# The delta net's 16 triangular systems substituted in two halves of eight, value units and doublings pinned between the steps

## The chip, the cores and the metric

The kernel runs on one core of one Trainium2 chip. A core has TensorE (PE, the matrix products; PEld is its weight load), VectorE (DVE), ScalarE (ACT), GpSimd (POOL) and SyncE (SP, which issues the loads). The engines run side by side and each works its own list of instructions strictly in order; an instruction that needs another engine's result waits on a semaphore, and everything behind it in its list waits too. The metric is the time of one execution on the device in microseconds (us), median of several runs.

## The reference, cut to what matters

Two blocks of a language model over 256 tokens of width 1024. The first has a state-space mixer and a mixture of experts; the second has four layers: attention with forget gates, gated linear attention, a gated delta net, and attention again. The change lies in the delta net alone:

```
qkv = silu(causal_conv(xn @ w_in))          # q, k: 4 heads of 128; v: 8 heads of 128
q = l2_norm(q) * d ** -0.5;  k = l2_norm(k)
tri = where(strict, (k*beta) @ k.T * decay, 0) + eye(64)     # per head and chunk of 64 tokens
u = triangular_solve(tri, v*beta);  w = triangular_solve(tri, k*beta*exp(gc))
# then a scan over the chunks, an RMS norm, a gate silu(z) and the output projection
```

The kernel treats the 256 tokens of a head as two blocks of 128, so there are 8 heads x 2 = 16 triangular systems of 128 x 128. Each needs an inverse.

## The kernel before, in words

Weights are streamed through a ring of six 1 MB slots in SBUF (`s.ring`). A unit of 256 output columns is split into a high and a low part (`split_unit`: ACT's cast at L247, DVE's subtraction at L248) and multiplied in three products per 128 rows and columns (`dense`, L277): 48 products of 128x256 per unit. The delta net (`gdn`, from L1458) takes its weights as such units: keys and queries (2, 0, 3, 1), values (4 to 7), the gate z (8, and a last one of 256 columns).

- `unit` (L1500) is one dense unit followed by a causal convolution of four taps and a silu (`conv_silu`: padding L352, ACT's first tap L356, six DVE steps L360, gating L365).
- `l2` (L1504) normalises keys and queries: sums by products with ones (L1510), inverse roots in 13 small steps (`rsqrt`, on POOL here), eight transposes that spread the roots (L1520), two scalings on DVE (L1522).
- `systems` (L1543) makes, for two groups of four systems, the key and query products (L1550), the decays (L336, L338 on PE, exponentials L343 on ACT) and the masked matrices U (L1560, L1561).
- `compact` (L1586) takes the 8x8 blocks of the diagonals out of U on DVE (L1589, L1591).
- `substitute` (L1593) inverts all 8x8 blocks of all 16 systems at once: ACT and POOL write the columns out wide (L1601), PE transposes them in seven transposes (L1604), DVE works seven steps of a product and a reduction (L1609, L1610), PE transposes back (L1612), ACT copies (L1613).
- `spread` (L1615) sets the blocks on the diagonals of Tm (L1618) and its transpose Vm by flips (L1581, copies L1621).
- `lower`, `update`, `flipped` (L1630 to L1660) double the size of the inverted blocks three times, 8 to 64. A level of a group of four systems is four products (L1636), a masked copy X on DVE (L1642), four products (L1654), an addition on DVE (L1655) and, on the first two levels, a flip (L1581) with a copy (L1660). The twelve level-and-group steps run as a pipeline, `lower` two ahead of `update` and three ahead of `flipped`.
- `queries` (L1537) multiplies the queries' decays by their products on DVE (L1539, L1540); `v_turn` (L1669) transposes the convolved values (L1672).

The program's text is not the order of the engines' lists. A scheduler with a timeline of its own sets the order of all instructions after their dependencies; `s.tc.issue_after(x)` is a further condition by which the instructions in it come behind x. In the order that it made, all four value units stand ahead of the second half's `systems` on PE.

## Time and profile before

| | us |
|---|---|
| median of 3 runs (1290.63 to 1292.61) | 1292.08 |
| profiled execution | 1291.23 |
| its span | 1289.6 |
| PE busy (88% of the span) | 1134.1 |
| DVE busy (46%) | 589.9 |
| ACT busy (38%) | 491.4 |
| POOL busy (11%) | 137.6 |
| mean granted TensorE clock, share of full | 0.965 |

The delta net takes the span from about 980 to 1155 us; `l2`, `systems`, the substitution and the doubling stand between 1003 and 1094. Shares over the whole span say little of such a stage; it is read from windows, from the timeline of an engine and from the chain of work that ended last. In a timeline, a row gives the start and the duration of a group of equal instructions, and in brackets for how long the engine was idle before it and whose result ended that. Instructions overlap by some 0.08 us on DVE, and matmuls are pipelined, so the time that one takes from the next is the distance of their starts.

### The profile page before, as it was taken

Reading aid. Unit: us, or ns where it says so; the run is one execution under the profiler, and the core shown is the slowest. Engines: PE = TensorE matmul, PEld = TensorE weight load, DVE = VectorE, ACT = ScalarE, POOL = GpSimd, SP = SyncE. Lnnn points to the kernel's source line nnn. Section 1 sums busy time; section 2 is a strip of 40 time slices with the busy share of each in tenths; the row PEclk is TensorE's granted clock in tenths of the full one; section 3 lists DMA queues with packets and bytes.
Section 4 is the critical chain, followed back from the end, with each engine's and each line's share of the span. In section 5 each row is a group of like instructions: output and inputs, shape, how many; then the busy total and the mean of one; then the engine's idle time right before and its main releaser. Section 6 shows DMA issues by size and latency. Waiting matters only on the chain.

```text
span 1289.6 us, 18973 instructions
## 1 busy us (share of the span) xinstructions
PE 1134.1 (88%) x7458; PEld 845.0 (66%) x7459; DVE 589.9 (46%) x1136; ACT 491.4 (38%) x996; POOL 137.6 (11%) x406
## 2 busy tenths in 40 slices
PE   5999999996778677777777999999999969999998
PEld 4998999741323131322314788989688959897887
DVE  3976776410101010110104565757467777666554
ACT  4554454210101010000104567656455533356763
POOL 2000632000000000000000332010001110012310
PEclk8999999998899898999989999999999979999999
DMA  6843647799999999999999553454335420165620
GB/s 226 290 134 99 191 159 283 280 421 425 421 424 424 425 424 424 425 425 424 425 424 317 171 164 131 166 165 153 112 109 170 138 76 2 34 165 168 158 98 33
DMA packets 126903, 312.72 MB, mean 242 GB/s; under 512 B 7559, under 2 KB 72842, under 8 KB 109530
## 3 DMA queue, kind: packets, MB, share of 16 engines
q1 hardware_dynamic: 126458, 311.26, 65.5%
q8 instruction: 60, 0.98, 0.3%
q0 software_dynamic: 352, 0.20, 0.1%
q14 instruction: 33, 0.27, 0.1%
HBM read 310.39 MB, written 1.05 MB: 242 GB/s over the span
## 4 chain that ended last, share of the span: by engine, by line
PE 39%; DMA 25%; DVE 3%; ACT 2%; issue 1%; POOL 1%; SPq 0%; DVEq 0%; ACTq 0%
PE pd L298 19%; DMA we<-in_w_down 12%; PE pd L277 9%; DMA we<-in_w_gate 6%; DMA we<-in_w_up 6%; DMA w<-in_fox_w_in 2%; DVE wl L248 1%; PE ps L1654 1%; PE ps L1193 1%; PE ps L1581 1%; PE ps L1636 1%; ACT wh L247 1%; PE ps L1211 1%; PE pd L969 1%; DVE cv L360 0%
## 5 line engine op out<-in xcount | busy, mean ns | idle before, releaser
L277 PE MATMUL pd<-x,wh 128*128 128x256 f32 x1744 | 327.6, 288 | 2.3 <-DVE x L161 1.2
L248 DVE TENSOR_TENSOR wl<-w,wh 128x1024 fp32r<-128x1024 f32 (+1 forms) x206 | 251.2, 1223 | 119.0 <-ACT wh L247 117.6
L247 ACT CAST wh<-w 128x1024 fp32r<-128x1024 f32 (+1 forms) x206 | 214.5, 1046 | 203.2 <-PE pd L277 103.8
L277 PEld LDWEIGHTS pd<-x,wh 128*128 128x128 f32 x1744 | 276.7, 194 | 5.5 <-DVE x L161 2.1
L298 PE MATMUL pd<-wh,x 128*128 128x512 f32 (+3 forms) x896 | 249.5, 367 | 6.9 <-ACT x L160 2.4
L277 PE MATMUL pd<-x,wl 128*128 128x256 f32 x872 | 248.8, 287 | 0.8 <-DVE wl L248 0.8
L969 PE MATMUL pd<-we,xt 128*32 128x512 f32 x1012 | 173.2, 681 | 71.9 <-DMA we<-in_w_up 50.6
L298 PEld LDWEIGHTS pd<-wh,x 128*128 128x128 f32 x896 | 159.7, 190 | 33.8 <-ACT wh L247 3.8
L277 PEld LDWEIGHTS pd<-x,wl 128*128 128x128 f32 x872 | 168.7, 194 | 1.6 <-DVE wl L248 1.3
L969 PEld LDWEIGHTS pd<-we,xt 128*32 128x32 f32 x1012 | 40.5, 122 | 195.7 <-DMA we<-in_w_up 86.8
L298 PE MATMUL pd<-wl,x 128*128 128x512 f32 (+3 forms) x448 | 158.3, 366 | 1.5 <-DVE wl L248 1.4
L993 PE MATMUL pd<-we,sq 128*32 128x512 f32 x512 | 98.2, 624 | 27.6 <-DMA we<-in_w_down 21.7
L298 PEld LDWEIGHTS pd<-wl,x 128*128 128x128 f32 x448 | 84.2, 190 | 15.6 <-DVE wl L248 2.9
L1005 DVE TENSOR_TENSOR hT<-hT,ps 128x512 f32<-128x512 f32 x32 | 22.0, 687 | 149.3 <-PE ps L1004 149.3
L993 PEld LDWEIGHTS pd<-we,sq 128*32 128x32 f32 x512 | 24.7, 112 | 94.0 <-issue 45.0
L982 DVE SCALAR_TENSOR_TENSOR cv<-cv,rslot,pd 128x512 f32<-128x512 f32 x8 | 6.0, 747 | 130.9 <-PE pd L969 130.9
L99 POOL TENSOR_SCALAR rq_y<-rs_v 128x8 int32<-128x8 int32 (+2 forms) x24 | 6.4, 266 | 522.8 <-DVE rs_v L192 440.0
L987 ACT COPY sq<-ps 128x512 f32<-128x512 f32 x8 | 4.7, 585 | 149.8 <-PE ps L985 149.8
L999 ACT COPY ys<-pd 128x512 f32<-128x512 f32 x16 | 9.3, 586 | 120.7 <-PE pd L993 120.7
L1316 POOL MEMSET at<- 128x1024 f32 x1 | 1.0, 951 | 434.7 <-PE pd L993 434.7
L980 DVE SCALAR_TENSOR_TENSOR cv<-th,pd 128x512 f32<-128x512 f32 x8 | 5.5, 688 | 85.8 <-ACT th L978 85.8
L978 ACT ACTIVATE th<-pd,rslot 128x512 f32<-128x512 f32 x8 | 5.5, 687 | 90.3 <-PE pd L969 51.3
(492 smaller groups left out, 1374.3 us busy)
## 6 DMA issues: line engine op xcount, KB each, us to landing
we<-in_w_down SPq DMA_DIRECT2D x46, 1024.0 KB, 14.8
we<-in_w_up SPq DMA_DIRECT2D x45, 1024.0 KB, 16.0
we<-in_w_gate SPq DMA_DIRECT2D x43, 1024.0 KB, 14.5
w<-in_fox_w_in SPq DMA_DIRECT2D x30, 1024.0 KB, 6.8
w<-in_w_in SPq DMA_DIRECT2D x22, 1024.0 KB, 7.7
we<-in_w_up SPq DMA_DIRECT2D x38, 512.0 KB, 14.2
we<-in_w_down SPq DMA_DIRECT2D x36, 512.0 KB, 15.8
we<-in_w_gate SPq DMA_DIRECT2D x34, 512.0 KB, 15.6
```

Of the source, the lines that this page charges most:

```text
L247: nc.scalar.copy(h, v[:, k:k + m])
L248: nc.vector.tensor_tensor(l, v[:, k:k + m], h, OP.subtract)
L277: nc.tensor.matmul(acc[:, c], w[k][:, cs], x[:, k, p], start=start and c == 0 and at == 0 and i == 0, stop=stop and at == KC - 1 and i == ...
L298: nc.tensor.matmul(acc[j], x[:, k, p, ts], w[k], start=k == order[0] and i == 0 and (n != T or j == 0), stop=k == order[-1] and i == 2, sk ...
L969: mm = nc.tensor.matmul(out[32 * j:32 * j + 32], xt[:, k, 32 * j:32 * j + 32], w[name, 4 * q + j, k // 4][k % 4], start=k == 0, stop=k == ...
L993: mm = nc.tensor.matmul(py[h][32 * j:32 * j + 32], at[:, f, 32 * j:32 * j + 32], w["w_down", 4 * q + j, f // 2][f % 2][:, 512 * h:512 * h ...
L1005: nc.vector.tensor_tensor(hT[:, 2 * u:2 * u + 2], hT[:, 2 * u:2 * u + 2], pt.rearrange("p (i t) -> p i t", i=2), OP.add)
L1193: nc.tensor.transpose(pt[:, (2 * i + j) * P:(2 * i + j + 1) * P], n4[w, j][:, 2 * o + i], s.ident)
L1211: nc.tensor.matmul(pl[:, P:384], q[:, P:], k, start=False, stop=False, skip_group_check=True)
L1581: nc.tensor.transpose(pt[:, a * P:(a + 1) * P], x[:, a], s.ident)
L1636: nc.tensor.matmul(pt[:, a * P:(a + 1) * P], U[:, 2 * g4 + a // 2, (a % 2) * P:(a % 2 + 1) * P], t[:, a], start=True, stop=True)
L1654: nc.tensor.matmul(pt[:, a * P:(a + 1) * P], l[:, a], m[:, a], start=True, stop=True)
```

## The change

`substitute(u, behind)` now works on one half, the eight systems of two groups: the columns are written wide by ACT alone (L1599) into a scratch X that is one slot of the weight ring, transposed to 64 partitions (L1605), copied to SBUF by ACT (L1606), and the seven steps of DVE (L1610, L1611) read them there. The transpose back is a function of its own, `substituted` (L1618). X also serves the doubling, one fixed buffer per group (L1646). The inverse roots of `l2` move from POOL to DVE. The program's text is rewritten so that the first half's substitution stands before the second half's `l2` and `systems`, and the second half's substitution beside the first half's three levels (`double`). `issue_after` pins: value unit 0 behind the last decay of the first half, the transposes behind that unit's last product (`s.mm`), value unit 1 behind the transposes, the transpose back behind unit 1; in the second half value unit 3 behind the last decay, the transposes behind it, and the transpose back behind the last product of `double(0, 2)`.

```diff
@@ dense
-                    nc.tensor.matmul(acc[:, c], w[k][:, cs], x[:, k, p], start=start and c == 0 and at == 0 and i == 0,
+                    s.mm = nc.tensor.matmul(acc[:, c], w[k][:, cs], x[:, k, p], start=start and c == 0 and at == 0 and i == 0,
...
@@ l2
+        s.quiet, quiet = nc.vector, s.quiet
         s.rsqrt(f, v, [P, 8])
+        s.quiet = quiet
...
+    room = s.ring.tile([P, KC * WIDE], F32, tag="w", name="X")[:, :2048].rearrange("p (u g a t) -> p u g a t", u=2, g=2, a=4)
+    X = [room[:, 0], room[:, 1]]
...
+    def substitute(u, behind):
+
+        mine = own[:, 8 * u:8 * u + 8]
+        nc.vector.tensor_tensor(mine, mine, s.eye8[:, None, :].to_broadcast([P, 8, 8]), OP.add)
+        t = s.tmp.tile([64, 16, 8], F32, tag="junk", name="rows8", bufs=1)
+        nc.vector.tensor_copy(t, s.eye8[:64, None, :].to_broadcast([64, 16, 8]))
+        flat = X[u].rearrange("p g a t -> p (g a t)")
+        wide = flat[:, 576:].rearrange("p (i a c) -> p i a c", i=7, a=8)
+        nc.scalar.copy(wide, mine[:, :, 1:].rearrange("p a i -> p i a")[:, :, :, None].to_broadcast([P, 7, 8, 8]))
+        rows_of = lambda i: flat[:64, (i - 1) * P:i * P]
+        for at, n in ((0, 4), (4, 3)):
+            pt = s.ps.tile([P, 512], F32, name="ps")
+            with s.tc.issue_after(behind):
+                for i in range(n):
+                    product[0] = nc.tensor.transpose(pt[:64, i * P:(i + 1) * P], wide[:, at + i].rearrange("p a c -> p (a c)"), s.ident).ins
+            nc.scalar.copy(flat[:64, at * P:(at + n) * P], pt[:64, :n * P])
         for i in range(1, 8):
...
+            m = rows_of(i).rearrange("p (n j) -> p n j", j=8)[:, :, :i + 1]
+            x = s.tmp.tile([64, 16, 8], F32, tag="E", name="terms")
...
+    def substituted(u, t, behind):
+        mine = own[:, 8 * u:8 * u + 8]
+        pt = s.ps.tile([P, 512], F32, name="ps")
+        with s.tc.issue_after(behind):
+            nc.tensor.transpose(pt[:, :64], t.rearrange("p n i -> p (n i)"), s.ident[:64, :64])
+        nc.scalar.copy(mine.rearrange("p a c -> p (a c)"), pt[:, :64])
...
-    for i in range(12 + 3):
-        if i < 12:
-            lower(i)
-        if 0 <= i - 2 < 12:
-            update(i - 2)
-        if 0 <= i - 3 < 12:
-            flipped(i - 3)
...
+    def double(u, lev):
+        for step in (lower, update, flipped):
+            for g4 in (2 * u, 2 * u + 1):
+                step(lev, g4)
...
+    q = unit(1)
+    systems(0, kn, qn)
+    pick(0)
+    with s.tc.issue_after(s.masked):
+        v_dense(0)
+    t = substitute(0, s.mm)
+    with s.tc.issue_after(product[0]):
+        v_dense(1)
+    substituted(0, t, s.mm)
+    kn, qn = l2(k, q)
+    v_dense(2)
+    end(0)
+    systems(1, kn, qn)
+    pick(1)
+    with s.tc.issue_after(s.masked):
+        v_dense(3)
+    t = substitute(1, s.mm)
+    for lev in range(3):
+        double(0, lev)
+    substituted(1, t, product[0])
     v_turn(0)
...
+    end(1)
+    double(1, 0)
+    v_turn(1)
+    for lev in (1, 2):
+        double(1, lev)
+        for g4 in (2 * lev - 2, 2 * lev - 1):
             with s.tc.issue_after(last[0]):
...
+                queries(g4)
+        v_turn(lev + 1)
```

In the rows of the engines' lists a name before the arrow is what is written, the names behind it what is read; `own` holds the 8x8 blocks, `sq` a block product of a group, `terms` and `rows8` belong to the substitution, `TV` holds Tm and Vm, `X` is the scratch, `pad` and `cv` belong to a convolution, `wl` is the low part of a weight unit.

Three places show what the scheduler made of it. The first is DVE's list before, at the end of the compaction of the last group, up to the first steps of the substitution:

```order
L1560 TENSOR_TENSOR U_8044<-Qd_8045,kk_8532 128x256
L1561 TENSOR_TENSOR U_8044<-Qx_8046,kk_8532 128x128
L1589 TENSOR_TENSOR sq_8567<-U_8044,block_1250 128x512
L1591 TENSOR_REDUCE own_8556<-sq_8567 128x32
L1595 TENSOR_TENSOR own_8556<-own_8556,eye8_1254 128x128
L1609 TENSOR_TENSOR terms_8586<-ps_8573,rows8_8571 128x16x2
L1610 TENSOR_REDUCE rows8_8571<-terms_8586 128x16
```

The same place in the first half of the change, from the last U to the end of the compaction, which is the row with `eye8`:

```order
L1564 TENSOR_TENSOR U_8044<-Qx_8046,kk_8431 128x128
L248 TENSOR_TENSOR wl_8516<-w_8509,wh_8515 128x1024
L361 SCALAR_TENSOR_TENSOR cv_8388<-pad_106,gconv_half_1271,cv_8388 128x256 x2
L1587 TENSOR_TENSOR sq_8457<-U_8044,block_1250 128x512
L361 SCALAR_TENSOR_TENSOR cv_8388<-pad_106,gconv_half_1271,cv_8388 128x256 x2
L1589 TENSOR_REDUCE own_8050<-sq_8457 128x32
L361 SCALAR_TENSOR_TENSOR cv_8388<-pad_106,gconv_half_1271,cv_8388 128x256 x2
L1594 TENSOR_TENSOR own_8050<-own_8050,eye8_1254 128x64
L353 TENSOR_TENSOR pad_106<-pd_8460,rstd_b_7861 128x2x256
L366 SCALAR_TENSOR_TENSOR cv_8388<-th_8397,cv_8388 128x512
```

Between the block products and the reductions of a group there now stand six steps of a convolution and a conversion of weights; the padding and the gating of convolutions come behind.

The second place is PE's list from the transposes of the substitution on, before:

```order
L1604 MATMUL ps_8573<-ident_79,wide_8575 128x128 x4
L1604 MATMUL ps_8574<-ident_79,wide_8581 128x128 x3
L1612 MATMUL ps_8607<-ident_79,rows8_8571 128x128
L1581 MATMUL ps_8755<-ident_79,TV_8047 128x128 x4
L1581 MATMUL ps_8762<-ident_79,TV_8047 128x128 x4
L1581 MATMUL ps_8769<-ident_79,TV_8047 128x128 x4
L1581 MATMUL ps_8776<-ident_79,TV_8047 128x128 x4
L1672 MATMUL ps_8782<-ident_79,cv_8670 128x128 x4
L1636 MATMUL ps_8788<-TV_8047,U_8044 128x128 x4
L1636 MATMUL ps_8868<-TV_8047,U_8044 128x128 x4
L1636 MATMUL ps_8876<-TV_8047,U_8044 128x128 x4
L1654 MATMUL ps_8884<-X_8793,TV_8047 128x128 x4
```

and in the second half of the change, from the last value unit's final product on:

```order
L277 MATMUL pd_8834<-x_7630,wl_8742 128x256
L1605 MATMUL ps_8910<-ident_79,X_8049 64x128 x4
L1605 MATMUL ps_8916<-ident_79,X_8049 64x128 x3
L1641 MATMUL ps_8942<-TV_8047,U_8044 128x128 x4
L1641 MATMUL ps_8949<-TV_8047,U_8044 128x128 x4
L1657 MATMUL ps_8956<-X_8049,TV_8047 128x128 x4
L1657 MATMUL ps_8962<-X_8049,TV_8047 128x128 x4
L1579 MATMUL ps_8968<-ident_79,TV_8047 128x128 x4
L1579 MATMUL ps_8974<-ident_79,TV_8047 128x128 x4
L1641 MATMUL ps_8980<-TV_8047,U_8044 128x128 x4
L1641 MATMUL ps_8987<-TV_8047,U_8044 128x128 x4
```

The doubling of the first half (L1641, L1657, L1579) now stands behind the transposes of the second, two groups at a time; before, the transpose back and the flips of all four groups followed at once.

The third is DVE's list in the second level of the doubling, before:

```order
L1540 TENSOR_TENSOR Qx_8046<-Qx_8046,qkp_8048 128x128
L360 SCALAR_TENSOR_TENSOR cv_9020<-pad_106,gconv_half_1271,cv_9020 128x256 x2
L1655 TENSOR_TENSOR TV_8047<-TV_8047,ps_8924 128x32x8
L360 SCALAR_TENSOR_TENSOR cv_9020<-pad_106,gconv_half_1271,cv_9020 128x256
L1642 TENSOR_TENSOR X_8945<-ps_8940,below_1242 128x16x16
L360 SCALAR_TENSOR_TENSOR cv_9020<-pad_106,gconv_half_1271,cv_9020 128x256
L1655 TENSOR_TENSOR TV_8047<-TV_8047,ps_8948 128x32x8
```

and in the change, in the second level of the second half, from the last X of the level to both additions:

```order
L361 SCALAR_TENSOR_TENSOR cv_8894<-pad_106,gconv_half_1271,cv_8894 128x256
L1542 TENSOR_TENSOR Qd_8045<-Qd_8045,qkp_8048 128x256
L1543 TENSOR_TENSOR Qx_8046<-Qx_8046,qkp_8048 128x128
L1746 COPY v_8051<-pd_9207 64x256
L1658 TENSOR_TENSOR TV_8047<-TV_8047,ps_9125 128x16x16
L361 SCALAR_TENSOR_TENSOR cv_8894<-pad_106,gconv_half_1271,cv_8894 128x256
L1658 TENSOR_TENSOR TV_8047<-TV_8047,ps_9131 128x16x16
```

Ahead of the seven rows of the change stand the last X of the level, three more pairs of `Qd` and `Qx` steps and a convolution step (order of the text: X, pairs, addition); before, two pairs stood between an X and an addition.

## Rows read from the trace of the kernel before

**Rows 1.** The windows of 20 us: stretch, length, then busy us and instructions of PE, PEld, DVE, ACT and POOL, the mean granted clock of PE as a share of full speed, the share of the DMA engines, GB/s.

```profile
1020.00:1040.00 20.00, 20.00 (x166) 19.39 (x165) 15.31 (x27) 11.17 (x19) 3.53 (x13) 1.00 0.39 132
1040.00:1060.00 20.00, 10.21 (x63) 7.90 (x62) 15.20 (x36) 6.99 (x19) 2.51 (x6) 0.75 0.28 54
1060.00:1080.00 20.00, 17.32 (x138) 16.57 (x137) 19.86 (x51) 9.45 (x19) 1.55 (x5) 0.91 0.00 1
1080.00:1100.00 20.00, 20.00 (x179) 19.09 (x179) 12.23 (x35) 4.50 (x11) 0.94 (x3) 1.00 0.01 2
```

**Rows 2.** PE's timeline: start, us, instruction and count, in brackets the idle time before it and who ended it.

```profile
1042.69 0.94 PE L1550 MATMUL ps<-k 128*128 128x128 f32 x6 [0.35 <-DVE k L1522]
...
1052.82 1.76 PE L1604 MATMUL ps<-ident,wide 128*128 128x128 f32 x7 [4.87 <-ACT wide L1601]
1057.91 0.48 PE L1612 MATMUL ps<-ident,rows 128*128 128x128 f32 x1 [3.33 <-DVE rows L1610]
1059.64 3.65 PE L1581 MATMUL ps<-ident,TV 128*128 128x128 f32 x16 [1.25 <-DVE TV L1618]
1065.22 0.66 PE L1672 MATMUL ps<-ident,cv 128*128 128x128 f32 x4 [1.93 <-DVE cv L365]
...
1068.74 1.13 PE L1654 MATMUL ps<-X,TV 128*128 128x128 f32 x8 [0.18 <-DVE X L1642]
...
1072.22 0.66 PE L1581 MATMUL ps<-ident,TV 128*128 128x128 f32 x4 [0.56 <-DVE TV L1655]
```

**Rows 3.** Windows of 1 us, columns as in the first group.

```profile
1050.00:1051.00 1.00, 0.00 (x0) 0.00 (x0) 0.96 (x3) 0.00 (x0) 0.00 (x0) 0.50 0.01 2
...
1063.00:1064.00 1.00, 0.28 (x2) 0.00 (x0) 0.97 (x3) 0.73 (x3) 0.00 (x0) 0.70 0.00 0
...
1122.00:1123.00 1.00, 1.00 (x7) 1.00 (x7) 1.00 (x5) 0.29 (x1) 0.00 (x0) 0.50 0.77 207
```

**Rows 4.** The chain of work that ended last, in order of time: start, us, instructions. The count of 32-bit products (L1510, L1636, L1654) is twice that of the program, since each is run in two passes; L277 and L1581 have one.

```profile
1003.38 1.68 PE ps L1510 x16
1005.07 7.06 PE pd L277 x58
...
1075.10 0.44 PE ps L1581 x4
1075.53 0.89 PE ps L1636 x8
1076.43 0.89 PE ps L1654 x8
...
1121.45 6.32 PE pd L277 x38
```

**Rows 5.** DVE's timeline in the second half's systems, the compaction, the spread and a convolution.

```profile
1041.94 0.69 DVE L1522 TENSOR_TENSOR k<-ps,cv 128x512 f32<-128x512 f32 x1 [1.13 <-PE ps L1520]
1042.55 0.68 DVE L1522 TENSOR_TENSOR q<-ps,cv 128x512 f32<-128x512 f32 x1
1043.15 1.22 DVE L248 TENSOR_TENSOR wl<-w,wh 128x1024 fp32r<-128x1024 f32 x1
1044.28 0.55 DVE L1554 TENSOR_TENSOR kk<-ps,strict 128x384 f32<-128x384 f32 x1
...
1047.49 0.55 DVE L1554 TENSOR_TENSOR kk<-ps,strict 128x384 f32<-128x384 f32 x1
1047.96 1.06 DVE L1591 TENSOR_REDUCE own<-sq 128x32 f32<-128x512 f32 x1
1048.94 0.41 DVE L1560 TENSOR_TENSOR U<-Qd,kk 128x256 f32<-128x256 f32 x1
...
1050.01 0.68 DVE L1589 TENSOR_TENSOR sq<-U,block 128x512 f32<-128x512 f32 x1
1050.73 1.07 DVE L1591 TENSOR_REDUCE own<-sq 128x32 f32<-128x512 f32 x1
1051.83 0.29 DVE L1595 TENSOR_TENSOR own<-own,eye 128x128 f32<-128x128 f32 x1
...
1058.80 2.50 DVE L1618 TENSOR_TENSOR TV<-own,block 128x512 f32<-128x512 f32 x4 [0.35 <-ACT own L1613]
1061.21 2.46 DVE L360 SCALAR_TENSOR_TENSOR cv<-pad,gconv_half,cv 128x256 f32<-128x256 f32 x6
```

**Rows 6.** ACT's timeline: the spread-out copy and the copy behind the transpose back.

```profile
1052.15 0.62 ACT L1601 COPY wide<-own 128x512 f32<-128x512 f32 x1 [3.08 <-DVE own L1595]
1058.50 0.27 ACT L1613 COPY own<-ps 128x128 f32<-128x128 f32 x1 [5.73 <-PE ps L1612]
```

**Rows 7.** DVE's timeline in the doubling: the query steps and a copy of 64 partitions.

```profile
1088.41 0.42 DVE L1539 TENSOR_TENSOR Qd<-Qd,qkp 128x256 f32<-128x256 f32 x1
...
1088.95 0.42 DVE L1539 TENSOR_TENSOR Qd<-Qd,qkp 128x256 f32<-128x256 f32 x1
...
1092.91 0.42 DVE L1718 COPY v<-pd 64x256 f32<-64x256 f32 x1
```

**Rows 8.** DVE's timeline in the later inverse roots of the delta net's result, which run on DVE before too.

```profile
1112.67 0.17 DVE L102 TENSOR_TENSOR rq_t<-rq_y 128x8 f32<-128x8 f32 x1
1112.87 0.17 DVE L104 SCALAR_TENSOR_TENSOR rq_t<-rq_t,rs_v 128x8 f32<-128x8 f32 x1
```

**Rows 9.** The page, part 6: DMA issues, with the median us from issue to landing.

```profile
w<-in_fox_w_in SPq DMA_DIRECT2D x30, 1024.0 KB, 6.8
```

74 lines of the change are left out of this document (23 added, 51 removed).

## The prediction

> **What bounds the kernel now.** The windows by stage come first: from 1040 to 1060 us TensorE (PE) works only 10.21 of 20 us, at a mean granted clock of 0.75, and from 1060 to 1080 it works 17.32 us at 0.91; the windows before and after are full [rows 1]. This hole is what the change bears on. PE's timeline says what each piece of it is [rows 2]: 4.87 us before the seven transposes of the substitution (L1604, released by ScalarE's spread-out copy), 3.33 before L1612 (the substitution itself on VectorE, DVE), 1.25 before the flips (L1581), 1.93 before the first value turn (L1672), then 0.18 and 0.56; 0.35 lies ahead of the second half's key products (L1550). Idle time in all: 12.47 us. The fine windows add the clock: at 1050 it is at 0.50 (1.2 GHz), PE having gone idle at 1047.95 (1052.82 less 4.87), and it is back at 1.00 only within 1063:1064 [rows 3]. The 16 flips took 3.65 us there; four take 0.44 later, so 16 would take 1.76 [rows 2, 4]: 1.9 lost. The seven transposes took 1.76 against about 0.95: 0.8 lost. **The hole is worth 15.2 us**, 1.2% of the profiled execution.
>
> Nothing fills it because the 48-product value units ran ahead: until 1041 PE was full, with L277 between everything else. The work is not missing, it was spent early. So the change can only redistribute: PE's total stays, and the question is whether the waits of the new order are shorter in sum.
>
> **The change, part by part.** Each half of eight systems now has its own chain: products and decays, compaction on DVE, ACT's spread-out copy, transposes, 14 DVE steps, a transpose back, spread, flips. Against a waiting piece one value unit is pinned: 48 products at 7.06 / 58 = 0.122 us, 5.84 us [rows 4]. What counts is how long DVE takes to the end of the compaction, because DVE works its list in order, and the order rows show conversions of weights (L248) and convolution steps (L361) between the steps of the chain.
>
> *First chain, to the transposes.* DVE's list from the key scaling k to the addition of the unit rows (L1594) holds, by the starts of neighbouring rows [rows 5]: k and q, 0.61 + 0.60; two L248 at 1.13, 2.26; twelve convolution steps at 2.46 / 6 = 0.41, 4.9; two kk at 0.47, 0.94; eight U in two sets of 1.07, 2.14; padding and gating (both 128x512, taken like q) 1.2; two block products and reductions, 0.60 (like q) + 0.98 and 0.72 + 1.10, 3.4; the addition 0.32. Sum 16.4. From there to the transposes 0.67 (1052.15 to 1052.82, [rows 2, 6]): 17.0 us after k starts. PE's cover from the same moment: the products begin 0.75 later (1041.94 to 1042.69), take 5.26 to the last mask at 1047.95, and the pinned unit adds 5.84: 11.85. **PE waits 5.2 us.** Before, the chain behind the second half's products left 4.87: the pinned unit buys nothing, since the convolutions of two earlier units stand in the same list. Behind the waiting L1605 in PE's queue stand the next units' products, ready long since, and all that follows.
>
> *Second chain, to the transposes.* The same list (twelve convolution steps and two L248 again). On PE eight flips (0.88) lie ahead of the products and hide the wait for k, so the cover is about 12.4: **4.6 us.**
>
> *The clock behind both.* A wait of 4.87 us brought it down in [rows 3], so I expect 0.50 behind each. Where the clock was low at 1122, 38 products took 6.32 us instead of 4.64, 1.7 lost [rows 3, 4]. Here 0.8 of that falls on the seven transposes, and of the rest only some 0.4 counts, since what follows waits for DVE anyway: 1.2 each, **2.4 us**; bounds 0 and 3.4. The trace shows the clock coming up behind the 16 flips, products with the identity, with nothing else on PE between 1059.64 and 1063.3. The Trainium skill ("TensorE: Matmul & The Clock Gate", Part 4: PE-mode transpose) says otherwise: transposes do not count as work that brings the clock up. By that the low stretch would outlast the seven transposes (7 x 0.22 us), half of that lost twice, 1.5 us more in the sum. I go by the trace.
>
> *The substitutions themselves.* Before, PE waited 3.33 us for the 14 steps. On 64 partitions from SBUF instead of 128 from PSUM I take the same time: a step of 64x256 takes 0.42, one of 128x256 0.42 [rows 7]; bounds 0 and 1 us less per half. In the first half 71 products (8.6 us) cover it: no wait. In the second, the doubling of the first half does.
>
> *The second normalisation.* PE goes from L1618 through the sums (1.68, [rows 4]) and the last 25 products of a unit (3.05): 4.7 us. DVE in that time must spread the first half (2 x 0.62, after ACT's 0.27), take the sums, do two L248 (2.26) and ten small steps of the roots at 0.20, each waiting for the one before [rows 5, 6, 8]: about 6.5 us. **PE waits 1.8 us** for the transposes of the roots (L1523).
>
> *The doubling.* Before, four groups of systems were in flight; a level costs a group 0.89 + 0.89 + 0.44 on PE [rows 4], and from 1080 on PE waited for nothing [rows 1], because three others' products lay between a group's steps. Now two are in flight, each step for both before the next step. First half: its X and T additions stand between the steps of the second substitution on DVE: waits of 0.4, 0.45 and 0.3, 1.2 in all. Handover: PE drains the transpose back (0.3), ACT copies (0.27), DVE spreads (0.62), with 0.44 of a value turn as cover and a second spread behind: 1.0. Second half, level 0: 0.9 (convolution steps ahead of X and the additions). Level 1: between the second group's X and the first group's addition DVE has four pairs of Qd and Qx, two convolution steps and a copy, 4 x 0.54 + 2 x 0.41 + 0.42 = 3.4 us [rows 5, 7], where PE has 0.9 of products: 2.4, and 0.3 for the next group. Level 2: 0.5. **6.3 us**; between 3 and 9, as each wait is a difference of two queues. Before, the same Qd and Qx steps hid under two other groups.
>
> *Additional.* Eight more transposes, 0.9; the first normalisation's scaling is no longer covered by L277, 0.7: **1.6 us.** SP issues the same loads in the same order, but the scratch X holds one of the six slots of the weight ring to the end of the doubling, so the first fox load goes out near 1100 instead of 1041. A load lands in 6.8 us [rows 9] and that one is wanted behind the output projection, so 0; at most 2, if a value unit's load were late with one slot less. POOL gives up the roots and zeroes one X per group, beside flips: 0.
>
> **Sum.** 5.2 + 4.6 + 2.4 + 1.8 + 6.3 + 1.6 = 21.9 in place of 15.2: +6.7 us, on the profiled execution's 1291.23 us 1297.9. The median of the runs lies 0.85 above that execution, so 1299 for a median. What follows (the values' solve, the projection) only shifts.
>
> **Rivals.** *It covers after all (faster).* If the compaction ends within 11.2 us of k in both halves, both long waits and the low clock go, 12.2 us: 1286.5. For it: without the convolutions and conversions ahead of L1594 the list is 9.2 us, and the pinned units then cover it. Against: the order rows put them ahead, and DVE's list runs in order. It is decided at L1605: PE's wait there under 1 us. *It nets out.* The clock stays up (-2.4) and the doubling costs half (-3.1): 1293.5, and with the transposes' and scaling's 1.6 hidden too, 1292. *Worse: the low clock lasts through the first half's doubling.* Its place is the 12.4 us of PE work there (two groups, three levels, no flips in the last), where PE stops for a moment at each step; at half clock it costs up to 12 more, of which DVE's interleaved steps hide half: 1305. For it: at 1122 the clock was low again after a few short stops [rows 3, 4]. Against: the flips in [rows 2] brought it up. The granted clock while double(0) runs decides.
>
> **How the numbers follow.** Forecast (1299, its own range 1294 to 1303) 0.62; covers 0.19; nets out 0.09; worse 0.10. A measurement here can tell about 0.2%, 2.6 us, from no change. Faster by more: 0.20 (the first rival and a sliver of the second); within: 0.09; slower: 0.71. The range 1286 to 1306 leaves out the better half of the first rival and the tail of the last.
>
> **What would show it.** In the profile of the changed kernel: PE idle 4 to 6 us before the first L1605 of each half, released by ACT's copy L1599, with DVE busy without a gap from k to L1594 (16 us); a clock of 0.50 behind both; 1.8 us before the second L1523, released by DVE; PE waits released by the additions L1658, the longest over 2 us in the second half's level 1; no PE wait before the first L1618. It is wrong if L1605 waits under 2 us in both halves, if k to L1594 takes under 13 us, or if PE waits for a weight load in 1010:1110.

## The result, and the profile after

The changed kernel takes 1308.84 us (median of 4 runs, 1306.58 to 1311.26) where the kernel before, on the same chip, takes 1291.39: a ratio of 1.0125, 95% interval 1.01 to 1.0151. (The ratios here and below are those on record for the fast runs; they differ a little from the quotient of the two medians, which is 1.0135 here.) It is slower, as forecast, but by about 17 us and not by 7: 2.8 us above the upper end of the range. The same kernel was timed a second time, against another set of runs of before: 1307.25 (1306.54 to 1308.28) against 1294.43, a ratio of 1.0115 (1.0084 to 1.0147).

The profiled execution took 1311.26 us. Its page, the span and the engines' busy time:

```profile
span 1309.6 us, 19000 instructions
...
PE 1148.9 (88%) x7466; PEld 854.2 (65%) x7467; DVE 596.1 (46%) x1172; ACT 493.6 (38%) x1002; POOL 128.2 (10%) x379
```

The span grew by 20.0 us. PE's busy time alone grew by 14.8 (1134.1 before), with eight more instructions: the same products took longer. So the first question is where, and the second at what clock.

**Cutting the span at landmarks.** Two instructions stand in both kernels on either side of the changed part: the padding of the first unit's convolution and the first scaling of the delta net's result `zs`. DVE's timeline, before:

```profile
981.36 0.68 DVE L352 TENSOR_TENSOR pad<-pd,rstd_b 128x512 f32<-128x512 f32 x1
...
1115.91 0.87 DVE L1770 SCALAR_TENSOR_TENSOR zs<-ps,fq,zs 128x128 f32<-128x128 f32 x3
```

and after:

```profile
987.84 0.69 DVE L353 TENSOR_TENSOR pad<-pd,rstd_b 128x512 f32<-128x512 f32 x1
...
1134.17 0.87 DVE L1798 SCALAR_TENSOR_TENSOR zs<-ps,fq,zs 128x128 f32<-128x128 f32 x3
```

From the first to the second row, called the stage from here on, it is 134.55 us before and 146.33 after: **+11.8**. Ahead of it stand +6.5 (987.84 less 981.36), where the program was not changed, and behind it +1.7 (span less the second landmark: 173.69 and 175.43). The second profile of the changed kernel has its padding at 983.23 and its `zs` at 1129.59, with a span of 1304.9: +1.9 ahead, +11.8 in the stage, +1.6 behind. The stage and what follows repeat, 13.4 to 13.5 us; what lies ahead does not.

**Ahead of the stage: the clock at two places, some 740 and 280 us earlier.** The windows of 240:260 (columns as in [rows 1]), before:

```profile
240.00:260.00 20.00, 19.36 (x167) 11.98 (x169) 9.45 (x55) 3.91 (x15) 2.83 (x13) 1.00 0.78 282
```

after:

```profile
240.00:260.00 20.00, 19.54 (x141) 13.16 (x141) 8.42 (x52) 3.03 (x11) 2.81 (x13) 0.83 0.66 231
```

and in the second profile of the same changed kernel:

```profile
240.00:260.00 20.00, 19.36 (x170) 11.98 (x173) 9.44 (x55) 3.85 (x15) 2.82 (x13) 1.00 0.77 285
```

The granted clock fell there in one execution and not in another of the same kernel; in the first profile PE is 3.0 us behind the kernel before at 247 us, and 3.0 again at 690; in the second it is not behind at either. The other 3.5 us come between 690 and 711 us, again with the clock. The windows of 700:720, before:

```profile
700.00:720.00 20.00, 18.40 (x104) 16.79 (x105) 14.46 (x30) 12.11 (x25) 4.29 (x13) 0.91 0.76 247
```

and after:

```profile
700.00:720.00 20.00, 13.76 (x77) 12.90 (x78) 13.28 (x24) 13.89 (x26) 0.39 (x2) 0.74 0.76 247
```

In the second profile the clock is 0.83 there, and it is 1.9 us behind. From 711 us to the padding nothing is added. Over the 14 profiles of this study the clock in 240:260 is 0.83 in five, whose padding starts at 985.4 to 987.8, and 1.00 in nine, whose padding starts at 980.3 to 983.9: on the mean 4.3 us apart. The instructions ahead of the padding stand in the same order on PE, DVE, ACT and POOL in all 14, and among the five is one kernel that is the one before with unread products added (e12_warm), among the nine are two with the halves of the change. So the bulk of it belongs to the execution. But four of the five are kernels with halves, and the two with halves among the nine have the latest paddings of those (983.2 and 983.9): that some 2 us of it belong to the change is not excluded.

**In the stage.** Windows of 20 us of the changed kernel, to be laid beside [rows 1]:

```profile
1020.00:1040.00 20.00, 14.88 (x95) 13.23 (x95) 18.17 (x44) 10.89 (x25) 0.32 (x1) 0.84 0.23 77
1040.00:1060.00 20.00, 17.35 (x128) 16.52 (x126) 12.90 (x33) 6.95 (x11) 0.31 (x1) 0.90 0.33 106
1060.00:1080.00 20.00, 15.19 (x105) 14.01 (x105) 17.02 (x42) 9.09 (x22) 0.62 (x2) 0.83 0.16 53
1080.00:1100.00 20.00, 19.17 (x163) 17.92 (x162) 12.48 (x31) 6.81 (x16) 1.87 (x6) 1.00 0.00 1
1100.00:1120.00 20.00, 17.68 (x128) 15.28 (x127) 13.34 (x39) 3.91 (x9) 0.62 (x2) 0.91 0.28 53
```

The one hole of before (10.21 us of work at 0.75) is gone; four shallow ones stand in its place, and each has its own dip of the clock. PE's timeline shows the waits, answering to [rows 2], and what a low clock does to the instructions behind them:

```profile
1034.74 1.70 PE L1605 MATMUL ps<-ident,X 128*64 128x128 f32 x7 [5.12 <-ACT X L1599]
...
1054.57 1.94 PE L1523 MATMUL ps<-ident,fl 128*128 128x128 f32 x8 [2.65 <-DVE fl L105]
1056.30 1.64 PE L1579 MATMUL ps<-ident,TV 128*128 128x128 f32 x8
...
1073.51 1.70 PE L1605 MATMUL ps<-ident,X 128*64 128x128 f32 x7 [4.81 <-ACT X L1599]
1075.00 3.38 PE L1641 MATMUL ps<-TV,U 128*128 128x128 f32 x16
...
1091.01 1.23 PE L1579 MATMUL ps<-ident,TV 128*128 128x128 f32 x8 [0.53 <-DVE TV L1624]
...
1104.10 1.43 PE L1579 MATMUL ps<-ident,TV 128*128 128x128 f32 x8 [2.15 <-DVE TV L1658]
1105.33 1.06 PE L1674 MATMUL ps<-ident,cv 128*128 128x128 f32 x4
1106.18 3.16 PE L1641 MATMUL ps<-TV,U 128*128 128x128 f32 x16
```

The waits are 5.12, 2.65, 4.81, 0.53 and 2.15 us. Windows of 1 us (columns as in [rows 1]) give the clock behind the four long ones:

```profile
1034.00:1035.00 1.00, 0.26 (x2) 0.22 (x3) 0.96 (x2) 0.69 (x3) 0.00 (x0) 0.50 0.12 40
1040.00:1041.00 1.00, 1.00 (x9) 1.00 (x8) 0.55 (x3) 0.00 (x0) 0.00 (x0) 0.77 0.00 0
...
1054.00:1055.00 1.00, 0.43 (x2) 0.46 (x3) 0.39 (x3) 0.00 (x0) 0.00 (x0) 0.55 0.96 341
1057.00:1058.00 1.00, 1.00 (x9) 1.00 (x7) 1.00 (x4) 0.93 (x3) 0.00 (x0) 0.74 0.00 0
1058.00:1059.00 1.00, 1.00 (x11) 1.00 (x10) 0.78 (x3) 0.56 (x1) 0.00 (x0) 1.00 0.00 0
...
1073.00:1074.00 1.00, 0.49 (x3) 0.43 (x4) 0.72 (x2) 0.45 (x1) 0.00 (x0) 0.50 0.01 2
1078.00:1079.00 1.00, 1.00 (x10) 1.00 (x10) 0.58 (x2) 0.00 (x0) 0.00 (x0) 1.00 0.00 0
...
1104.00:1105.00 1.00, 0.83 (x6) 0.59 (x7) 0.77 (x3) 0.52 (x1) 0.00 (x0) 1.00 0.00 0
1105.00:1106.00 1.00, 1.00 (x8) 1.00 (x8) 0.69 (x1) 0.74 (x3) 0.00 (x0) 0.65 0.00 0
1107.00:1108.00 1.00, 1.00 (x7) 1.00 (x6) 0.00 (x0) 0.01 (x1) 0.00 (x0) 0.50 0.00 0
1109.00:1110.00 1.00, 1.00 (x12) 1.00 (x11) 0.55 (x2) 0.00 (x0) 0.00 (x0) 1.00 0.00 0
```

It is at 0.50 (1.2 GHz) behind each of the four, the waits of 2.65 and 2.15 us too. At the last the wait was over at 1104.10, the clock still 1.00 in that microsecond, and it fell only in the next ones, when PE was full: a window with PE at 1.00 busy and the clock at 0.50 is pure loss.

**Behind the stage, +1.7.** The largest piece is one wait. In the last layer PE's first products after a normalisation, before:

```profile
1166.37 1.19 PE L298 MATMUL pd<-wh,x 128*128 128x512 f32 x4 [0.85 <-ACT wh L247]
```

and after:

```profile
1185.44 1.19 PE L299 MATMUL pd<-wh,x 128*128 128x512 f32 x4 [2.25 <-ACT wh L247]
```

They wait for ACT's cast of a weight, 1.4 us longer. ACT's timeline after shows what is queued in front of the cast:

```profile
1182.39 0.37 ACT L1180 ACTIVATE junk<-pd,rstd 128x128 f32<-128x128 f32 x1 [1.52 <-PE pd L299]
...
1182.89 0.37 ACT L1180 ACTIVATE junk<-pd,rstd 128x128 f32<-128x128 f32 x1
...
1183.38 0.37 ACT L1180 ACTIVATE junk<-pd,rstd 128x128 f32<-128x128 f32 x1
...
1183.73 0.36 ACT L138 COPY rstd_b<-ps 128x256 f32<-128x256 f32 x1
1183.99 0.38 ACT L1180 ACTIVATE junk<-pd,rstd 128x128 f32<-128x128 f32 x1
...
1184.34 2.00 ACT L247 CAST wh<-w 128x1024 fp32r<-128x1024 f32 x2
```

Four squares and a copy; in the trace of before the copy and one square stood in front of the same cast. No line of that layer was edited: the scheduler ordered the whole program anew. The clock is at 0.50 behind this wait too (in 1188:1189, with PE at 1.00 busy), as it is at this place in all six profiles of kernels with halves: a fifth piece of the same kind. In turn the changed kernel lacks the low clock that [rows 3] shows at 1122, and the two about cancel.

### The profile page after: what moved, and what is told of

It reads as the page before. It is cut to its first block, busy times and chain, and to the rows that moved or that the text cites. A ratio compares the mean times of both kernels' runs of the same rounds, so it can differ in the third digit from the quotient of the medians.

```text
span 1309.6 us, 19000 instructions
## 1 busy us (share of the span) xinstructions
PE 1148.9 (88%) x7466; PEld 854.2 (65%) x7467; DVE 596.1 (46%) x1172; ACT 493.6 (38%) x1002; POOL 128.2 (10%) x379
## 4 chain that ended last, share of the span: by engine, by line
PE 58%; DMA 32%; DVE 5%; ACT 2%; issue 1%; POOL 1%; SPq 0%; DVEq 0%; ACTq 0%; POOLq 0%
PE pd L277 21%; PE pd L299 20%; DMA we<-in_w_down 12%; DMA we<-in_w_up 9%; DMA we<-in_w_gate 8%; DMA w<-in_fox_w_in 2%; PE pd L970 2%; DVE wl L248 1%; DMA rows<-in_ssd_conv_w 1%; DVE cv L361 1%; PE ps L1641 1%; ACT wh L247 1%; PE ps L185 1%; PE pd L994 1%; PE ps L1194 1%
## 5 line engine op out<-in xcount | busy, mean ns | idle before, releaser
L277 PE MATMUL pd<-x,wh 128*128 128x256 f32 x1744 | 326.8, 288 | 3.4 <-DVE x L161 1.6
L277 PEld LDWEIGHTS pd<-x,wh 128*128 128x128 f32 x1744 | 276.1, 194 | 6.7 <-DVE x L161 2.4
L277 PE MATMUL pd<-x,wl 128*128 128x256 f32 x872 | 248.0, 286 | 1.2 <-DVE wl L248 1.2
L299 PEld LDWEIGHTS pd<-wh,x 128*128 128x128 f32 x896 | 161.6, 192 | 37.9 <-ACT x L160 5.3
L277 PEld LDWEIGHTS pd<-x,wl 128*128 128x128 f32 x872 | 168.4, 194 | 2.3 <-DVE wl L248 1.9
L299 PEld LDWEIGHTS pd<-wl,x 128*128 128x128 f32 x448 | 84.8, 192 | 15.7 <-DVE wl L248 2.8
## 6 DMA issues: line engine op xcount, KB each, us to landing
we<-in_w_down SPq DMA_DIRECT2D x46, 1024.0 KB, 14.8
```

The costliest lines, as they stand in the source:

```text
L277: s.mm = nc.tensor.matmul(acc[:, c], w[k][:, cs], x[:, k, p], start=start and c == 0 and at == 0 and i == 0, stop=stop and at == KC - 1 an ...
L299: nc.tensor.matmul(acc[j], x[:, k, p, ts], w[k], start=k == order[0] and i == 0 and (n != T or j == 0), stop=k == order[-1] and i == 2, sk ...
```

## The experiments

Three questions: what makes the two long waits, what the low clock behind all four costs, and whether the halves themselves or the pins and the moved roots make the kernel slower. Unread products below are `keep_warm`, a function that both kernels have: products of constants of 128x256 in bf16 that nothing reads, some 0.115 us each (2.56 us for 22). Stage lengths are between the two landmarks, as above, and so leave out what lies ahead.

| run | kernel | median us | before's median | ratio (95%) | stage us |
|---|---|---|---|---|---|
| | before | | | | 134.55 |
| | changed | 1308.84 | 1291.39 | 1.0125 (1.01 to 1.0151) | 146.33 |
| e7_again | changed, again | 1307.25 | 1294.43 | 1.0115 (1.0084 to 1.0147) | 146.36 |
| e1_late | changed, convolutions late | 1302.67 | 1291.76 | 1.0065 (1.004 to 1.009) | 139.46 |
| e2_warm | changed, two waits filled | 1304.73 | 1291.76 | 1.0078 (1.0052 to 1.0103) | 142.44 |
| e6_warm | changed, four filled, 38 at the roots | 1305.38 | 1294.43 | 1.0092 (1.0058 to 1.0125) | 141.41 |
| e8_warm | changed, four filled, 15 at the roots | 1302.78 | 1293.21 | 1.007 (1.0045 to 1.0095) | 139.04 |
| e3_slot | before, X in a ring slot | 1290.88 | 1291.76 | 0.9998 (0.9978 to 1.0019) | 134.97 |
| e4_whole | before, roots and pins | 1291.42 | 1291.76 | 0.9984 (0.9969 to 1.0) | 136.57 |
| e5_three | e4_whole, two units free, convolutions late | 1293.91 | 1294.43 | 1.0006 (0.9988 to 1.0024) | 135.61 |
| e9_pool | before, conversions on GpSimd | 1299.92 | 1293.21 | 1.0052 (1.0032 to 1.0071) | 140.07 |
| e10_both | e5_three, conversions on GpSimd | 1293.69 | 1293.21 | 1.0011 (0.9992 to 1.0029) | 136.10 |
| e11_warm | e4_whole, its three waits filled | 1291.86 | 1291.58 | 0.9994 (0.998 to 1.0008) | 132.74 |
| e12_warm | before, its two long waits filled | 1295.16 | 1291.58 | 1.0008 (0.9991 to 1.0024) | 133.81 |

**e1_late: the convolutions behind the compaction.** In the changed kernel the convolutions of the units that come between are issued only after the addition that ends the half's compaction.

```diff
-    def unit(u):
+    def unit(u, late=False):
...
+        def conv():
+            return s.conv_silu(None, pq, rb2, ...
+        return conv if late else conv()
...
+        made[2] = nc.vector.tensor_tensor(mine, mine, s.eye8[:, None, :].to_broadcast([P, 8, 8]), OP.add).ins
...
-    k = unit(3)
+    k = unit(3, True)
...
     t = substitute(0, s.mm)
+    k, q = k(), q()
...
     t = substitute(1, s.mm)
+    for i in range(4):
+        vc[i] = vc[i]()
```

> Theory A (VectorE's list): both long waits before L1605 come from the convolution steps that stand between the steps of the chain in VectorE's list. With the convolutions of units 3 and 1 behind the first half's addition of the unit rows, and those of the value units behind the second's, the list from the key scaling to that addition falls from 15.7 us to about 10, the wait before the transposes from 5.1 and 4.8 us to under 1 each, and the clock stays at 1.00 behind them: 9.9 less 1 for the waits, and about half of the 4.6 us that the low clock takes from the transposes, the 71 products and the first L1641: 1297 us (1293 to 1301). Theory B (the chain itself): the chain's products, decays and copies need those 16 us, and the convolutions only fill VectorE's pauses: the waits stay over 4 us and the time at 1306 to 1311.

Measured: 1302.67 us, the stage 6.9 us shorter than the changed kernel's. From k to the addition DVE takes 11.1 us instead of 15.7, and PE's timeline shows the first long wait gone:

```profile
1025.77 0.96 PE L1607 MATMUL ps<-ident,X 128*64 128x128 f32 x7 [0.15 <-ACT X L1601]
...
1041.80 0.27 PE L1620 MATMUL ps<-ident,rows 64*128 64x64 f32 x1 [3.56 <-DVE rows L1613]
```

The second is 1.53 for 4.81. So it was mostly the convolutions in DVE's list that made the waits, as the forecast said; the transposes behind the first take 0.96 us, the full clock. But the convolutions have to stand somewhere: they now come between the 14 steps of the substitution, and the transpose back waits 3.56 us where it waited for nothing, with the clock at 0.50 behind it. Of the 11.8 us that were expected the stage gives 6.9, and the kernel stays slower than before.

**e2_warm: the two long waits filled.** Nothing waits less here by design; PE only computes unread products while it waits.

```diff
-    t = substitute(0, s.mm)
+    t = substitute(0, s.keep_warm(s.mm, 40).ins)
...
-    t = substitute(1, s.mm)
+    t = substitute(1, s.keep_warm(s.mm, 38).ins)
```

> 40 and 38 products whose result nobody reads stand in TensorE's queue ahead of the transposes of the two halves, 4.7 and 4.5 us of work inside the two waits. Theory D (the clock is a cost of its own): the granted clock stays at 1.00 behind both, the seven transposes take 0.95 us instead of 1.70, the products behind the first 8.7 instead of 10.3, the first L1641 1.8 instead of 3.2; 3 to 5 us come back: 1304 to 1306. Rival: what TensorE loses at the low clock is hidden behind VectorE anyway; the next wait (before the second L1523) grows by what is won, and the time stays within 1 us of the changed kernel's 1308.8.

Measured: 1304.73 us, the stage 3.9 us shorter. The clock behind the first wait, and behind the wait for the roots, which was not filled:

```profile
1034.00:1035.00 1.00, 1.00 (x10) 1.00 (x10) 0.59 (x4) 1.00 (x3) 0.00 (x0) 1.00 0.00 0
1051.00:1052.00 1.00, 1.00 (x7) 1.00 (x6) 0.26 (x1) 0.00 (x0) 0.00 (x0) 0.50 0.00 0
```

The first is at 1.00 now. The low clock behind two waits costs 3.9 us, and behind the roots' wait it is still at 0.50.

**e3_slot: the ring slot alone**, in the kernel before.

```diff
+    room = s.ring.tile([P, KC * WIDE], F32, tag="w", name="X")[:, :2048].rearrange("p (g a t) -> p g a t", g=4, a=4)
...
-        X[i] = s.tmp.tile([P, 4, P], F32, tag="kq"[i % 2], name="X")
+        X[i] = room[:, g4]
```

> The kernel before, with its scratch X in a slot of the weight ring from the same place on as in the changed kernel. Theory C (the slot): a slot less moves weight loads, and the 6.5 us by which the changed kernel is late before its own stage begins come from it; this kernel then shows the same lateness (the padding of unit 2 at 988 us instead of 981) and is slower by 3 to 7 us, 1294 to 1298. Rival (chance of the execution): the same within 0.2% of 1291.4.

Measured: 1290.88 us, a ratio of 0.9998 (0.9978 to 1.0019), the stage 134.97. The slot costs nothing that can be measured.

**e4_whole: the roots on DVE and pinned value units, with one substitution of all 16 systems**, from the kernel before.

```diff
+        s.quiet, quiet = nc.vector, s.quiet
         s.rsqrt(f, v, [P, 8])
+        s.quiet = quiet
...
+            with s.tc.issue_after(s.mm):
+                for i in range(n):
+                    flips = nc.tensor.transpose(pts[c][:, i * P:(i + 1) * P], ...
+        with s.tc.issue_after(flips):
+            v_dense(1)
...
+    with s.tc.issue_after(s.masked):
+        v_dense(0)
     substitute()
-    v_dense(0)
-    v_dense(1)
```

> The kernel before with one substitution of sixteen systems kept, and the other two parts of the change done: the roots on VectorE and the first two value units pinned, one behind the last mask, one behind the substitution's transposes. Theory A: VectorE's list from the first key scaling to the addition is about 27 us, TensorE has 19 us of work in that time, so it waits about 8 us in one or two pieces ahead of the transposes, and none in the substitution; the doubling keeps its four groups in flight. 15.2 us of hole become about 10 with the clock: 1287 (1283 to 1293). Rival (the pins and the roots are what costs, not the halves): 1298 or more.

Measured: 1291.42 us, the ratio 0.9984 (0.9969 to 1.0): not slower than before. Its stage is 2.0 us longer in the profile. PE's timeline shows what the pins did:

```profile
1020.04 1.87 PE L1510 MATMUL ps<-ones,sq 128*128 128x1 f32 x8 [3.72 <-ACT sq L1506]
...
1023.80 1.86 PE L1510 MATMUL ps<-ones,sq 128*128 128x1 f32 x8 [1.90 <-ACT sq L1506]
...
1028.91 1.94 PE L1522 MATMUL ps<-ident,fl 128*128 128x128 f32 x8 [3.24 <-DVE fl L105]
```

The units now cover the substitution, and are missing at the second normalisation, ahead of it. The hole has moved and costs about the same. So the roots on DVE and two pinned units do not by themselves make a kernel slower. What is left are the halves, with their two compactions, two waits and a doubling two groups wide; that is an elimination, since no run has the halves without their pins.

**e5_three: more cover ahead of the second normalisation**, from e4_whole: two value units free, two pinned, the convolutions late.

```diff
         with s.tc.issue_after(flips):
-            v_dense(1)
+            v_dense(3)
...
+    v_dense(0)
+    v_dense(1)
     with s.tc.issue_after(s.masked):
-        v_dense(0)
+        v_dense(2)
     substitute()
+    for i in range(4):
+        vc[i] = vc[i]()
```

> One substitution of sixteen systems, roots on VectorE, as the run with the whole substitution; but the first two value units are free to run where that run waited for the second half's sums and roots (3.72, 1.90 and 3.24 us, with the clock at 0.54 in 1020:1040), the third is pinned behind the last mask and the fourth behind the substitution's transposes; their convolutions come after the substitution. Theory A (a pinned unit pays where VectorE's list ahead of the chain is free of convolutions and four groups stay in flight): the three waits ahead go, the one before the transposes stays under 5 us, none is left before the transpose back: 1283 (1279 to 1288). Rival (the work is only moved again, and the wait grows elsewhere by what is filled): 1290 to 1294.

Measured: 1293.91 us, a ratio of 1.0006 (0.9988 to 1.0024). The waits in the stage are 1.6 for the sums, 3.3 for the roots, 1.6 for the transposes, 2.9 for the flips and 2.2 for the first value turn. From the first k to the addition DVE takes 37.0 us, 34.2 in e4_whole and 38.9 before. The hole only moved again.

**e6_warm and e8_warm: all four waits filled.** To e2_warm are added unread products at the roots and at the second half's level 1, and value unit 2 stands ahead of the sums. The two differ in the number at the roots.

```diff
+        behind = s.keep_warm(ss, n).ins if n else None
...
+            warm = s.keep_warm(product[0], 18).ins if step is flipped and (u, lev) == (1, 1) else None
...
-    kn, qn = l2(k, q)
     v_dense(2)
+    kn, qn = l2(k, q, 38)
```

> The changed kernel with products that nobody reads in four waits: before both rows of L1605, before the second half's L1523 (with the third value unit ahead of the sums), and before the second half's flips at level 1. Theory D: the clock stays at 1.00 from 1030 to 1110, and besides the 4.1 us that the first two gave back, the transposes of the roots and the flips behind them (1.94 and 1.64 us at the low clock instead of 0.87 and 0.88) and the first products of level 2 (1.9 lost) come back: 1301 to 1303. Rival: VectorE's waits grow by as much: 1304.7 again, as with the two alone.

Measured: 1305.38 us, the stage 141.41. 38 were too many: the roots were ready at 1049.6, and k was scaled only at 1053.21. With 15 in place of 38:

> The run with four filled waits, but with 15 unread products before the second half's L1523 instead of 38, since 38 kept TensorE busy about 2.7 us past the moment when the roots were ready. Counted from the padding of unit 2 to the first scaling of the result, the changed kernel takes 146.3 us, with the first two waits filled 142.4, with all four and the 38 products 141.4. Theory D (the low clock, not the waits, is the undersized term): 138.5 to 139.5, so the low clock costs 7 to 8 us where the sum had 2.4. Rival: VectorE sets the end of each of these pieces, and it stays at 141 to 142.4.

Measured: 1302.78 us, the stage 139.04, 7.3 us shorter than the changed kernel's. The instructions that the changed kernel ran at half speed now run at full speed, as PE's timeline shows:

```profile
1068.66 0.96 PE L1607 MATMUL ps<-ident,X 128*64 128x128 f32 x7 [0.87 <-ACT X L1601]
1069.45 1.95 PE L1643 MATMUL ps<-TV,U 128*128 128x128 f32 x16
```

0.96 for 1.70 and 1.95 for 3.38. By this the low clock of the changed kernel costs some 7.3 us; the move of value unit 2 is in that figure too. It is not all of the clock's cost, for at the roots the clock falls here as well, as in e6_warm, with no wait: behind the sixteen sums of one column (L1511, 1045.80 to 1047.64) it is at 0.50, with PE full:

```profile
1048.00:1049.00 1.00, 1.00 (x7) 0.70 (x6) 0.86 (x7) 0.00 (x0) 0.00 (x0) 0.50 1.08 384
```

The transposes of the roots take 1.52 us, 1.94 in the changed kernel and 1.03 at the full clock. So at this place the wait is not the only thing that brings the clock down. What is left against before, 4.5 us of stage, are the waits, since the unread products fill them and shorten none.

**e7_again: the changed kernel once more**, with no edit.

> The changed kernel once more, for the 6.5 us by which its profiled execution was late before its own stage began. If that is chance of the execution, the padding of unit 2 (first L353 of the stage) comes anywhere between 978 and 988 us, and the median of the runs falls to about 1305; if it belongs to the program, it comes at 984 to 988 again and the median stays at 1307 to 1310.

Measured: 1307.25 us; what lies ahead of the stage fell from +6.5 to +1.9, the rest is the same to 0.1 us. The two signs disagree: the padding, at 983.23, came as chance would have it, the median as if the time belonged to the program. Before's own median was 1294.43 beside it, 3.0 above that of the first comparison, so the medians do not decide it.

**e9_pool: the value units' conversions on GpSimd**, in the kernel before, to relieve DVE's list.

```diff
-                nc.vector.tensor_tensor(l, v[:, k:k + m], h, OP.subtract)
+                s.low.tensor_tensor(l, v[:, k:k + m], h, OP.subtract)
...
+        s.low = nc.gpsimd
         vc[u] = unit(4 + u)
+        s.low = nc.vector
```

> The kernel before; only the subtraction that makes the low parts of the value units' weights (L248, eight of 1.13 us on VectorE) goes to GpSimd, whose 128x256 casts take 1.2 us. Theory E (VectorE's list bounds the stage from the first key scaling to the doubling): 9 us leave that list, of which the second normalisation's wait takes part; the second key scaling comes some 3 us earlier, and the run ends at 1287 to 1290, 2 to 5 us below before. Rival (GpSimd is late or disturbs VectorE): the products of the value units wait for it, 1293 to 1300.

Measured: 1299.92 us, a ratio of 1.0052 (1.0032 to 1.0071): slower. GpSimd takes 2.4 us for a conversion where DVE takes 1.13, and the roots, which before stand on GpSimd too, queue behind the conversions. PE's timeline has the new wait:

```profile
1046.11 1.42 PE L1520 MATMUL ps<-ident,fl 128*128 128x128 f32 x8 [3.97 <-POOL fl L109]
```

**e10_both: the same conversions on GpSimd in e5_three**, whose roots are on DVE. The edit is that of e9_pool.

> The run with one substitution, two free and two pinned value units, and the value units' low parts on GpSimd as well. Theory E: from the first key scaling to the addition of the unit rows that run took 37.0 us with six subtractions of 1.13 in VectorE's list; without them about 31, the pinned units still fill the wait before the transposes and the substitution: 1283 (1280 to 1288). Rival: GpSimd's subtractions come too late for the pinned units and TensorE waits for them: 1290 or more.

Measured: 1293.69 us, a ratio of 1.0011 (0.9992 to 1.0029), no gain. DVE's list has fewer steps, but they are held: from the first k to the addition it takes 37.9 us, 37.0 in e5_three. DVE's timeline at the end of the compaction:

```profile
1050.07 2.47 DVE L1599 TENSOR_TENSOR own<-own,eye 128x128 f32<-128x128 f32 x1
```

and GpSimd's at the same time:

```profile
1050.01 2.39 POOL L248 TENSOR_TENSOR wl<-w,wh 128x1024 fp32r<-128x1024 f32 x1 [13.91 <-ACT wh L247]
```

The addition takes 0.29 in [rows 5]; beside the conversion it takes 2.47, and ends 0.14 us after it.

**e11_warm: e4_whole with its three waits filled** by 28, 13 and 24 unread products.

```diff
+        behind = s.keep_warm(s.masked, 28).ins if n[0] else None
...
+            behind = s.keep_warm(ss.ins, n[w]).ins if n[0] else None
...
-    kn, qn = l2(k, q)
+    kn, qn = l2(k, q, (13, 24))
```

> The run with one whole substitution, and 28, 13 and 24 unread products in its three waits ahead of the second key scaling (3.72, 1.90 and 3.24 us; the clock was at 0.54 in 1020:1040). Theory D: the transposes of the roots and the second half's products run at the full clock (0.87 instead of 1.94 us; the four groups of six products, 6.2 us, in 3.3), and some 3 to 4 us of that lie on the way to the addition of the unit rows: 1288 (1286 to 1290) where that run had 1291.4. Rival: VectorE sets the end there, 1290.5 to 1292.5.

Measured: the stage 132.74, 3.8 us shorter than e4_whole's and 1.8 shorter than before's: the shortest of all. The run time, 1291.86 us against 1291.58, ratio 0.9994 (0.998 to 1.0008), cannot be told from before's.

**e12_warm: the kernel before with its two long waits filled** by 38 and 26.

```diff
+            if c == 0:
+                warm = s.keep_warm(s.masked, 38).ins
...
+        warm = s.keep_warm(flips, 26).ins
```

> The kernel before, with 38 and 26 unread products in its two longest waits (4.87 us before the seven transposes, 3.33 before the transpose back). Theory D: the transposes take 0.95 us instead of 1.76 and the sixteen flips 1.8 instead of 3.65; 1 to 2.7 us come back, as the wait for the convolution behind the flips (1.93) takes up part of the flips' gain: 1290 to 1292 beside 1292 to 1294 for the kernel before, a ratio of 0.998 to 0.9992. Rival: VectorE has no pause from the spreading on, so that only the transposes' 0.8 can count: 0.9992 to 1.0005.

Measured: a ratio of 1.0008 (0.9991 to 1.0024), the stage only 0.7 us shorter. The transposes take 0.98 instead of 1.76 us, but the 16 flips still 3.36, at a clock of 0.50 in 1065:1066, with waits of 1.25 before and 2.12 behind them that were not filled. No kernel of the study beats the one before by more than a measurement here can tell.

## Why the prediction was right in sign and too small in size

*What held.* Nothing can be gained because the cover had been spent early: e4_whole and e5_three show it best, in which the hole turns up at another place whenever units are moved. The first wait was put at 5.2 and is 5.12, the second at 4.6 and is 4.81. Its cause held: DVE runs from k at 1017.78 to L1594 at 1033.47 without a wait, 15.7 us where 16 were said, and with the convolutions taken out of that stretch (e1_late) the first wait falls to 0.15. The chain goes through the convolution itself at its end: its last two steps on DVE release a `th` on ACT (L364, 0.63 us), which stands ahead of the spread-out copy (L1599) in ACT's list. The ring slot at 0 is right (e3_slot), the eight transposes are there (7466 products for 7458), no wait stands before the first L1618, and none for a load in the stage.

*The step that failed: "the clock behind both", 2.4 us, with bounds of 0 and 3.4.* It is some 7.3 us by e8_warm. By rows of the changed kernel, each against the same instructions at full speed, it is 7.8: 2.4 behind the first wait (the transposes 1.70 for 0.95, and 71 products of L277, 10.31 in the chain of work that ended last, for 8.66 at 0.122 each), 1.5 behind the roots' wait (1.94 for 1.03, and 1.64 for 1.04), 2.2 behind the second (the transposes again, and L1641 3.38 for 1.95), 1.7 behind that of level 1 (1.06 for 0.60, L1641 3.16 for 1.95). Two things were wrong in it. It counted two waits and there are four: [rows 3] showed a fall behind a wait of 4.87 us, and also a low clock at 1122 behind a few short stops; the second was not carried over to the waits of 1.8 and 2.4 us that the same sum had listed. And it said that of what follows the transposes "only some 0.4 counts, since what follows waits for DVE anyway"; behind the transposes PE had its products ready, and most of what they lost at half clock was on the path: for the two waits alone e2_warm gives back 3.9 of the 4.6 that the rows show, above the upper bound. The third rival had the mechanism, low clock during the first half's doubling, but its place was wrong: the clock is back at 1.00 by 1078, 3 us into that doubling, and the loss is spread over four places.

*By the sum.* In the stage it comes to +11.8 where +6.7 was said. PE's waits in the forecast are 18.6 in place of 12.47, +6.1; the profile has PE idle for 17.75 in place of 14.05 in the stage, +3.7, and 2.1 more that neither clock nor transposes explain and that may be short gaps beneath the modelled ends of products: +5.8. The clock makes +5.1 (7.8 in place of 2.7) where the forecast has it unchanged, −0.3. The transposes are put at +0.9 in both. So, if those 2.1 are waits, the waits together were a little too large, and the clock is the whole of the miss.

*Within the waits.* Roots 2.65 for 1.8, 0.85 too little: between two steps of the roots DVE has a conversion that waits 0.89 us for ACT's cast, where the forecast counted two conversions without a wait.

```profile
1052.92 1.23 DVE L248 TENSOR_TENSOR wl<-w,wh 128x1024 fp32r<-128x1024 f32 x1 [0.89 <-ACT wh L247]
```

Level 1 of the second half 2.15 for 2.4; the handover 0.53 for 1.0; the doubling in all 3.05 for 6.3, or about 5 if those 2.1 belong there. That the sum of the waits came out close is in part luck: one term too small, another too large.

*The second step that failed: "what follows only shifts".* +1.7 us, with the 1.4 in the last layer the largest piece. Five of the six profiles of kernels with halves have 175.2 to 175.5 us from the second landmark to the end, e6_warm's 176.7; the others have 171.9 to 172.5, but for the kernel before and e12_warm, which have the low clock of [rows 3] in that stretch, at 173.7. Against the rest the tail is some 3 us longer. The forecast had followed the engines' lists only around the change.

*What brings the clock up.* From 1054.57 to 1057.78 PE ran only the 16 transposes of L1523 and L1579, and the granted clock came up meanwhile: 0.55 in 1054:1055, 0.74 in 1057:1058, 1.00 in the next. The Trainium skill ("TensorE: Matmul & The Clock Gate", Part 4: PE-mode transpose) does not count transposes as work that brings it up; this trace disagrees, as that of before did, and the forecast's choice to go by the trace was right.

*What belongs to neither.* Of the 17 us between the medians (13 against the second set of runs of before) 13.5 are the kernel's own by two profiles. With the clock (5.4 more) and the last layer (1.7) right the same sum would have read 6.7 + 5.4 + 1.7 = 13.8 above the profiled execution, 1306 for a median. The rest is, in the profiles, what lies ahead of the stage; most of that differs from one execution to the next.

*Still open:* whether some 2 us ahead of the stage belong to the change, what the 2.1 us above are, what brings the clock down at the roots beside the wait, and whether a schedule exists in which DVE's convolutions stand neither ahead of the compaction nor in the substitution; e1_late moved them once, further places were not tried.

## What to carry to other kernels

When a wait is cut into several, price the clock behind each piece, not only behind the long ones: here four waits of 14.7 us in all cost some 7.3 us more in products at half speed, and the profile shows it as busy time. Before pinning work into a wait, ask where that work was cover until now, and what stands in the list of the engine that ends the wait. And compare two profiles from landmark to landmark, since what lies ahead of the change need not be the same in both.

## What the hardware showed that was not expected

The granted clock fell behind waits of 2.65 and 2.15 us, and behind the second only after the wait was over, while PE was full. At the place of the first it fell in e6_warm and e8_warm too, where no wait was left and PE had just run sums of one column. 40 and 38 unread products held it at 1.00 through two waits of about 5 us, and two such waits then cost 3.9 us less.

The same instructions ahead of the stage took up to 7.5 us more in one profile than in another (paddings at 980.31 and 987.84). Between the profile of before and the first of the changed kernel, 6.5 us apart, 3.0 came with a granted clock of 0.83 for 1.00 in 240:260 and 3.5 with 0.74 for 0.91 in 700:720.

A conversion of 128x1024 on GpSimd (2.4 us) holds a short step of DVE that starts beside it: 2.47 us for 0.29, and in the same profile 2.51 for a gating of 0.69. The small steps of the substitution beside another conversion (1054.30 to 1056.70) were not held: 0.20 to 0.28.
